# Where in SyncE's queue 32 loads for the gate rows of a two-layer diffusion block stand

## The chip, the core and the metric

The kernel runs on one core of one Trainium2 chip. The metric is the device time of one execution in microseconds (us), taken from several runs; beside it, one execution was recorded by the hardware profiler, and its span is the time from the first to the last instruction. In the rows of the profile PE is TensorE's matmuls, PEld its weight loads, DVE is VectorE, ACT is ScalarE, POOL is GpSimd and SP is SyncE; SPq and ACTq are the DMA queues that SyncE and ScalarE issue to. L439 is line 439 of the kernel.

## The reference

The reference is a small diffusion backbone of two layers over 256 latent tokens and 256 context tokens of width 1024, in float32. Each layer has a token mixer (a convolution module in layer 0, a bidirectional chunkwise mLSTM in layer 1) and a squared-ReLU MLP; each sub-layer is modulated, gated and normed. The modulation comes from one matrix per layer, applied to the latent condition `c` and to a learned context vector `c_ctx`:

```python
def adaln(cvec, w, b):
    return jnp.split(jax.nn.silu(cvec) @ w + b, 6, axis=-1)

for i in range(DEPTH):
    sh1, sc1, g1, sh2, sc2, g2 = adaln(c[:, None, :], ada_w[i], ada_b[i])
    csh1, csc1, cg1, csh2, csc2, cg2 = adaln(c_ctx, ada_w[i], ada_b[i])
    u, uc = modulate(h, sh1, sc1), modulate(hc, csh1, csc1)
    ...
    h = layer_norm(ALPHA * h + g1 * y, ln1_g[i], ln1_b[i])
    h = layer_norm(ALPHA * h + g2 * sq_relu_mlp(modulate(h, sh2, sc2), mlp_w1[i], mlp_w2[i]), ln2_g[i], ln2_b[i])
```

In layer 1 the mixer forms queries and keys from a convolved stream `xc`, values from `xm`, gates from all three, and an output gate `o`; then come attention over chunks, a norm per head, a down projection and the MLP. Layer 1 gives only the latent stream out, so of its gates only `g1` and `g2` of the latent condition are used. These two vectors of 1024 numbers are the "gate rows".

## The kernel before

**Products.** Weights arrive in blocks of 128 rows x 2048 columns of float32 (1 MB) by `raw_load` (L147 to L150) into one of three `raw` buffers. Each half of a block is split by `split_w` into a rounded high part (ScalarE's cast, `wh`, L155) and a remainder (VectorE's subtraction, `wl`, L156); four buffers of each exist. A product is three matmuls (high by high, high by low, low by high: L186, L189, L190; with other operand order L228 to L230). In the second layer's query stage it is two matmuls with operands side by side (L202). `raw_load` notes its DMA in `loaded[0]`: at any place of the program text that name stands for the weight load (or readback) written last.

**Stages around the change.** The MLP of layer 0 runs in four parts `c` of 1024 hidden columns: w1 in eight steps of 128 columns over 512 tokens, then relu on ScalarE (L1207), square on VectorE (L1208) and a split into `hid`; then w2, which adds into `x`. In the last part w2 runs over one half of the tokens after the other and keeps its later weights in `u` tiles. After it come the z and x halves of the up projection (`up_z`, `up_x`), the values (`wv`), and for each of two pairs of heads the queries (`queries`, `wq`) and the keys (`pair`, `wk`). In the keys each step of 128 rows is multiplied by the queries, split into `rr`, and one step later used by the scores (L1492 to L1497). Then come the output gate (`wo`), attention and the rest.

**The sums for the modulation of layer 1.** They are not matmuls. `AdaV` (L417 to L449) loads a block `adaT_w[unit, b, half]` of 128 columns of the modulation by 512 inputs (256 KB) into one of two `ar` buffers (L445, L446), and VectorE multiplies it by a broadcast row of silu(condition) and sums along the row in one instruction (L439), starting from the bias for the first half and from the first half's sum for the second. A unit is 512 columns, so it needs 8 loads. `ada_n1` sums four units for both conditions and is stepped in the MLP of layer 0. `ada_n2` sums eight units for the latent condition alone, in the order (6, 7, 8, 9, 4, 5, 10, 11): first shift and scale of the second sub-layer, then units 4, 5 (`g1`) and 10, 11 (`g2`). That makes 64 loads, numbered by `i`, and `n = i // 8`. Its steps are written into the program text at these places: 32 in the loop of `wv`, 4 in the queries of each head, 8 in the keys of each pair, and one at the end, after which `gate_rows` (L1255 to L1257) stores the two gate rows from their columns to DRAM, each as 1024 single numbers in another order. They are read back as rows, the first into `G` (L1650).

**What sets the order.** The framework that builds the kernel gives each engine its own list of instructions. It plans that order itself, from priorities that follow the program text and from its own estimate of when operands and buffers are ready; an instruction that is ready early may be placed far ahead of its place in the text. On the chip each engine then works its list in order and waits where an operand or buffer isn't ready. Two aids bind the plan: `tc.keep_in_program_order(ins)`, and `with tc.issue_after(ins):`, which puts the instructions of its block behind `ins` on the same engine's list. SyncE's list holds nearly all loads, weights and `ar` alike.

Of the kernel before, what the change touches and what calls it, by code (L numbers as in the profile page):

```python
# [71 lines left out]
def hybrid_kernel(ctx: ExitStack, tc: tile.TileContext, xT, vecs_d, taps_d, bdw_d, ada0_w, ada_w, adaT_w, wg_d, pw1a, pw1, pw2, w1_0, w2_0,  # L72
                  w1_1, w2_1, up_x, up_z, wv, wo, bo_d, wk, wq, wqT, wdown, rows_d, out):
    nc = tc.nc
# [10 lines left out]
    def nm(s):  # L85
        uid[0] += 1
        return f"{s}_{uid[0]}"
# [64 lines left out]
    loaded = [None]  # L152
# [9 lines left out]
    def split_w(src, make=None):  # L162
        n = src.shape[-1]
        if make is not None:
            his, los = [], []
            for i in range(0, n, T):
                his.append(make(F32R))
                los.append(make(F32R))
                split(his[-1], los[-1], src[:, i:i + T])
            return his, los  # L170
        hi = wp.tile([P, 1024], F32R, tag="wh", name=nm("wh"), bufs=NW)[:, :n]
        lo = wp.tile([P, 1024], F32R, tag="wl", name=nm("wl"), bufs=NW)[:, :n]
        anchors.append(split(hi, lo, src))
        return hi, lo
# [242 lines left out]
    class AdaV:  # L417
# [25 lines left out]
        def load(self):  # L443
            n, kt = divmod(self.i, DT)
            w = adp.tile([P, 512], F32, tag="ar", name=nm("ar"), bufs=2)  # L445
            nc.sync.dma_start(w, adaT_w[self.units[n], kt // 2, kt % 2])  # L446
            self.i += 1
            return w

# [1382 lines left out]
    def down(h):  # L1832
# [21 lines left out]
        if h == 0:  # L1854
            for hf, ws in enumerate(load()):
                for t in range(2):
                    ps = psum(("fl", "ln")[t])
                    mms(ps, ws, hf, t, True, True)
                    e_ = tmp("E")
                    nc.vector.tensor_tensor(e_, ps, G1[:, HF[hf]], op=ALU.mult)  # L1860
                    nc.vector.tensor_tensor(R[:, t, HF[hf]], R[:, t, HF[hf]], e_, op=ALU.add)
                    yield
        elif h < H - 1:
            if h == 1:
                acc.extend([[psum(), psum("fl")], [psum(), psum()]])
            for hf, ws in enumerate(load()):
                for t in range(2):
                    mms(acc[t][hf], ws, hf, t, h == 1, False)
                    yield
        else:  # L1870
            for t in range(2):
                for hf in range(2):
                    mms(acc[t][hf], pre3, hf, t, False, True)
                    with tc.issue_after(normed[0]) if t else nullcontext():
                        residual(t, hf, acc[t][hf], G1)
                    yield
                if t == 0:
                    normed.append(ln1_rows(0))
# [191 lines left out]
    for c in range(4):  # L2070
# [24 lines left out]
        for k2 in range(4):  # L2095
            raw = raw_load(w2_1[4 * c + k2])
            for i in range(2):
                kt = 2 * k2 + i
# [3 lines left out]
                w = split_w(raw[:, i * 1024:(i + 1) * 1024])  # L2102
                w = [[w_[:, sl] for sl in HF] for w_ in w]
# [127 lines left out]
```

## Time and profile before

| what | us |
|---|---|
| median of 3 runs | 1650.22 (1646.95 to 1651.23) |
| profiled execution | 1650.45 |
| its span | 1648.7 |
| 96 `ar` loads issued, first and last | 164.8 and 509.9 |
| 16 `wq` and 16 `wk` loads, median to landing | 4.8 |
| `ar` loads, median to landing | 3.0 |

The mean granted clock of TensorE over the span is 0.992. The stages in the order of time: layer 0's mixer to about 213 us, its MLP to about 585 us, the up projection to about 740 us, values to 912 us, queries and keys of the first pair to 1044 us, of the second to 1188 us, then output gate, attention, down projection and the MLP of layer 1.

A page of the profile names a group of instructions by line, engine, operation and its tiles (written tile, arrow, read tiles). In an order of time each row starts with the start and the length in us, and a bracket at its end gives the idle time of the engine before it and what released it. A row of windows gives the length, busy time and count of each engine, then the granted clock (1.00 is full speed), the share of the 16 DMA engines in use and GB/s. Although the steps of `ada_n2` are written into the values, queries and keys, the last of its loads was issued at 509.9 us, in the MLP of layer 0: the plan had placed them as soon as their operands were there.

### The profile page before, as it was taken

The page shows a single profiled execution, that of the slowest core. Times are in us where ns is not written, and L with a number is a line of the kernel's source. Part 1 is how long each engine was busy: PE and PEld are TensorE (multiplying, and loading weights), DVE is VectorE, ACT ScalarE, POOL GpSimd, SP SyncE. Part 2 cuts the span into 40 slices and gives each one's busy share as a digit, 9 for nine tenths or more (in the row PEclk, how much of TensorE's full clock was granted, in tenths as well). Part 3 has the DMA queues.
Part 4 walks back from the last instruction along what each step waited for, and adds up shares of the span by engine and source line. Part 5 has one row for each costly group of instructions (what it writes and reads, how often), then busy time and mean ns, then how long its engine had stood idle before and what let it go on. Part 6 is the DMA issues. An engine that isn't in the chain of part 4 may idle for free.

```text
span 1648.7 us, 22836 instructions
## 1 busy us (share of the span) xinstructions
PE 1623.7 (98%) x8754; PEld 1356.6 (82%) x8754; DVE 1077.0 (65%) x2052; ACT 728.1 (44%) x1173; POOL 15.2 (1%) x67
## 2 busy tenths in 40 slices
PE   9999999999996999999999999999999999999998
PEld 6675998888885998887777899898888888888887
DVE  7697886986756676763233643453389876787777
ACT  4214763322314376652222532442378654555453
POOL 0000000000000000000000000000000000000001
PEclk9999999999998999999999999999999999999999
DMA  9766233555655157578654632343375566745552
GB/s 361 250 220 239 103 115 128 197 190 193 201 176 153 52 164 226 188 242 281 220 188 149 238 128 103 107 175 131 136 258 187 209 230 203 255 182 190 191 192 90
DMA packets 91069, 306.88 MB, mean 186 GB/s; under 512 B 15020, under 2 KB 33360, under 8 KB 63312
## 3 DMA queue, kind: packets, MB, share of 16 engines
q1 hardware_dynamic: 66416, 289.12, 50.2%
q10 hardware_dynamic: 24544, 16.30, 3.2%
q8 instruction: 69, 1.13, 0.3%
q14 instruction: 40, 0.33, 0.1%
HBM read 287.52 MB, written 17.87 MB: 185 GB/s over the span
## 4 chain that ended last, share of the span: by engine, by line
PE 90%; DMA 6%; DVE 3%; issue 1%; ACT 0%; DVEq 0%; SPq 0%; ACTq 0%
PE mm L186 15%; PE mm L189 15%; PE mm L190 15%; PE mm L202 10%; DMA ar<-adaT_w 4%; PE mm L228 4%; PE mm L230 3%; PE mm L229 3%; PE cv L230 2%; PE cv L228 2%; PE cv L229 2%; PE fl L360 1%; DMA raw<-w 1%; DVE ar L439 1%; PE ln L228 1%; PE ln L229 1%
## 5 line engine op out<-in xcount | busy, mean ns | idle before, releaser
L156 DVE TENSOR_TENSOR wl<-raw,wh 128x1024 fp32r<-128x1024 f32 (+1 forms) x344 | 416.5, 1215 | 255.4 <-ACT wh L155 250.5
L155 ACT CAST wh<-raw 128x1024 fp32r<-128x1024 f32 (+1 forms) x344 | 357.0, 1045 | 458.8 <-PE mm L189 269.0
L189 PE MATMUL mm<-u,wh 128*128 128x512 f32 (+1 forms) x802 | 288.7, 361 | 0.0
L186 PE MATMUL mm<-u,wh 128*128 128x512 f32 (+1 forms) x674 | 239.3, 356 | 0.0
L190 PE MATMUL mm<-u,wl 128*128 128x512 f32 (+1 forms) x674 | 238.1, 355 | 0.0
L189 PEld LDWEIGHTS mm<-u,wh 128*128 128x128 f32 x802 | 151.2, 189 | 23.0 <-issue 0.8
L186 PEld LDWEIGHTS mm<-u,wh 128*128 128x128 f32 x674 | 127.2, 189 | 20.5 <-issue 2.4
L190 PEld LDWEIGHTS mm<-u,wl 128*128 128x128 f32 x674 | 127.1, 189 | 18.5 <-issue 0.8
L186 PE MATMUL mm<-hid,wh 128*128 128x512 f32 (+1 forms) x256 | 95.1, 372 | 13.4 <-ACT hid L155 13.3
L186 PE MATMUL mm<-xm,wh 128*128 128x512 f32 x256 | 100.2, 391 | 0.0
L190 PE MATMUL mm<-xm,wl 128*128 128x512 f32 x256 | 99.6, 389 | 0.0
L189 PE MATMUL mm<-hid,wh 128*128 128x512 f32 (+1 forms) x256 | 94.8, 370 | 0.7 <-DVE hid L156 0.7
L190 PE MATMUL mm<-hid,wl 128*128 128x512 f32 (+1 forms) x256 | 94.5, 369 | 0.0
L228 PE MATMUL mm<-wh,xl 128*128 128x512 f32 x208 | 81.5, 392 | 1.0 <-ACT xl L155 1.0
L229 PE MATMUL mm<-wh,xl 128*128 128x512 f32 x208 | 81.2, 390 | 0.0
L230 PE MATMUL mm<-wl,xl 128*128 128x512 f32 x208 | 80.4, 391 | 0.0
L189 PE MATMUL mm<-qq,wh 128*128 128x272 f32 x256 | 73.9, 289 | 0.0
L186 PE MATMUL mm<-qq,wh 128*128 128x272 f32 x256 | 73.5, 288 | 0.0
L190 PE MATMUL mm<-qq,wl 128*128 128x272 f32 x256 | 73.5, 288 | 0.0
L186 PEld LDWEIGHTS mm<-hid,wh 128*128 128x128 f32 x256 | 50.1, 196 | 21.6 <-ACT hid L155 14.1
L1373 DVE SCALAR_TENSOR_TENSOR E<-pad,vecs,E 128x512 f32<-128x512 f32 x64 | 48.0, 750 | 27.3 <-ACT E L1371 26.0
L155 ACT CAST hid<-E 128x256 fp32r<-128x256 f32 (+1 forms) x70 | 33.9, 485 | 67.9 <-DVE E L1208 64.4
(595 smaller groups left out, 3245.9 us busy)
## 6 DMA issues: line engine op xcount, KB each, us to landing
raw<-w SPq DMA_DIRECT2D x64, 1024.0 KB, 4.9
raw<-wo SPq DMA_DIRECT2D x32, 1024.0 KB, 4.9
ar<-adaT_w SPq DMA_DIRECT2D x96, 256.0 KB, 3.0
raw<-ada_w SPq DMA_DIRECT2D x20, 1024.0 KB, 7.4
raw<-wv SPq DMA_DIRECT2D x16, 1024.0 KB, 6.3
raw<-wq SPq DMA_DIRECT2D x16, 1024.0 KB, 4.8
raw<-wk SPq DMA_DIRECT2D x16, 1024.0 KB, 4.8
u<-wqT SPq DMA_DIRECT2D x56, 256.0 KB, 5.7
```

What stands on the lines that cost most here:

```text
L155: c = nc.scalar.copy(hi, src)
L156: lastsub[0] = nc.vector.tensor_tensor(lo, src, hi.bitcast(F32), op=ALU.subtract).ins
L186: a = nc.tensor.matmul(ps, wh, xh, start=start, stop=False)
L189: nc.tensor.matmul(ps, wh, xl, start=False, stop=False)
L190: lastmm[0] = nc.tensor.matmul(ps, wl, xh, start=False, stop=stop).ins
L202: nc.tensor.matmul(o_, w_, x_, start=start and i == 0, stop=stop and i == 15)
L228: nc.tensor.matmul(ps, xh, wh, start=start, stop=False)
L229: nc.tensor.matmul(ps, xl, wh, start=False, stop=False)
L230: return nc.tensor.matmul(ps, xh, wl, start=False, stop=stop).ins
L360: a = mark_unit[0] = nc.tensor.matmul(ps[32 * j:32 * j + 32], cs[:, kt, 14 - 2 * v:46 - 2 * v], blocks[kt], start=first and kt < 4, stop=l ...
L439: nc.vector.tensor_tensor_reduce(tmp("S") if s == 0 else w, w, crow[s][half], 1.0, o if half else V(f"ada_b{self.l}", col), op0=ALU.mult, ...
L1373: nc.vector.scalar_tensor_tensor(s2_(acc), pad[:, :, k:k + C], V("w_conv", m * QTAP + k), s2_(acc), op0=ALU.mult, op1=ALU.add)
```

## The change

```diff
         def load(self):
             n, kt = divmod(self.i, DT)
             w = adp.tile([P, 512], F32, tag="ar", name=nm("ar"), bufs=2)
-            nc.sync.dma_start(w, adaT_w[self.units[n], kt // 2, kt % 2])
+            with tc.issue_after(loaded[0]) if n > 3 else nullcontext():
+                nc.sync.dma_start(w, adaT_w[self.units[n], kt // 2, kt % 2])
             self.i += 1
             return w
```

`n > 3` never holds for `ada_n1`, which has four units. For `ada_n2` it holds for the last 32 loads, those of units 4, 5, 10 and 11. Each of them is placed on SyncE's list behind the load that `raw_load` wrote last before it in the program text. The load with `i = 32` is written in the last step of `wv`; those with `i` from 33 to 63 are written one per step in the queries and keys, so that behind nearly every `wq` and `wk` load comes one `ar` load. No instruction is added or removed, and the first 32 loads of `ada_n2` are bound to nothing, as before.

## The prediction

> **What bounds the kernel now.** I read the page's busy row and its slices first, to see whether one engine sets the time.
>
> ```profile
> span 1648.7 us, 22836 instructions
> ...
> PE 1623.7 (98%) x8754; PEld 1356.6 (82%) x8754; DVE 1077.0 (65%) x2052; ACT 728.1 (44%) x1173; POOL 15.2 (1%) x67
> ...
> PE   9999999999996999999999999999999999999998
> ```
>
> TensorE is busy in 98% of the span. A slice is 1648.7/40 = 41.2 us, and before the last only the thirteenth (494.6 to 535.8 us) is below 9. What can be won lies there. Two windows of the stages and two of TensorE alone say how much (busy time by engine, then granted clock, DMA share, GB/s):
>
> ```profile
> 428.00:519.00 91.00, 91.00 (x409) 75.56 (x408) 59.59 (x120) 25.05 (x33) 0.00 (x0) 1.00 0.57 183
> 519.00:545.00 26.00, 11.91 (x59) 10.72 (x58) 10.20 (x18) 6.82 (x11) 0.00 (x0) 0.61 0.59 162
> ```
>
> ```profile
> 521.00:533.00 12.00, 0.00 (x0) 0.60 0.75 172
> 533.00:535.00 2.00, 1.64 (x6) 0.50 0.02 8
> ```
>
> Up to 519 us TensorE never idles; then come 12 us without a matmul, and work resumes at a granted clock of 0.50. The view of TensorE's waits (total, times, longest) and its order of time name the cause:
>
> ```profile
> PE mm L186 <- ACT hid L155: 13.3, 2, 12.1
> PE mm L189 <- DVE hid L156: 0.7, 2, 0.3
> ```
>
> ```profile
> 533.04 0.58 PE L186 MATMUL mm<-hid,wh 128*128 128x256 f32 x1 [12.10 <-ACT hid L155]
> ...
> 537.67 0.58 PE L186 MATMUL mm<-hid,wh 128*128 128x256 f32 x1 [1.23 <-ACT hid L155]
> ...
> 543.38 0.41 PE L189 MATMUL mm<-hid,wh 128*128 128x256 f32 x1
> 543.60 0.37 PE L190 MATMUL mm<-hid,wl 128*128 128x256 f32 x1
> 543.80 0.28 PE L186 MATMUL mm<-hid,wh 128*128 128x256 f32 x1
> 543.92 0.28 PE L189 MATMUL mm<-hid,wh 128*128 128x256 f32 x1
> ```
>
> This is the start of the first layer's last w2 product, and it lacks the last blocks of hid. ScalarE makes them, and its queue stood at the cast of a weight load that had landed late; SyncE's queue shows why that load was issued late (x counts the loads of a row):
>
> ```profile
> 531.34 1.14 ACT L155 CAST u<-raw 128x512 fp32r<-128x512 f32 x2 [10.23 <-DMA raw<-w]
> ```
>
> ```profile
> L446 SPq DMA_DIRECT2D ar<-adaT_w x96: 327/328/425, 164.8 to 509.9; - x96
> ```
>
> ```profile
> 426.14 10.07 SPq L446 DMA_DIRECT2D ar<-adaT_w  x5
> ...
> 496.63 9.85 SPq L446 DMA_DIRECT2D ar<-adaT_w  x5
> 507.28 0.33 SPq L149 DMA_DIRECT2D raw<-w  x1
> 508.55 1.71 SPq L446 DMA_DIRECT2D ar<-adaT_w  x2
> 518.43 0.33 SPq L149 DMA_DIRECT2D raw<-w  x1
> ```
>
> Between weight loads stand up to five ar loads. Each waits for one of two ar buffers, so for a reduce on VectorE, which waits for an ar load in turn: five take 10 us, and the weights queue behind them. Counted back from the last of the 96, at 509.9 us, the 32 that the change moves begin with the group of 426.14 us (its first is the 64th or 65th of all). The whole stretch before the hole is theirs. The weight load of 518.43 us was slow besides:
>
> ```profile
> raw<-w SPq DMA_DIRECT2D x1, 1024.0 KB, 12.8
> raw<-up_z SPq DMA_DIRECT2D x1, 1024.0 KB, 14.1
> g_dr<-ada ACTq DMA_DIRECT2D x1, 4.0 KB, 11.1
> ```
>
> ```profile
> 516.70:527.80 11.10, 3.80 (x23) 3.00 (x22) 5.43 (x7) 2.27 (x4) 0.00 (x0) 0.80 0.50 28
> ```
>
> The first fence is the DMA view from 516 to 532 us (KB, us to landing), the second a window over the store of the second gate row. These 4 KB take 11.1 us, in which all DMA together moves 28 GB/s, against 183 in the stretch before; the load beside it landed after 12.8 us.
>
> **The change part by part.** It adds no instruction and removes none. It ties 32 loads of 256 KB to weight loads of the second layer: the first to the last load of the wv stage, the others to those of wq and wk (some to a readback of xc between them). Their 32 reduces move with them and, as they need the sums, the two stores.
>
> *What goes.* The waits: 13.3 + 0.7 = 14.0 us. The slow clock: it ends between 543.60 and 543.80, where the step from matmul to matmul falls from 0.22 to 0.12 us. From 533.04 to 543.6 are 10.6 us; less the 1.5 us of the later waits (13.3 + 0.7 without the 12.1 and one 0.3) they are 9.1, and the same matmuls at full clock save 9.1 x (1 - 0.12/0.22) = 4.1 us. Together 18 us, the most that can go.
>
> *What is late next.* A step of w1 is 24 matmuls of 0.22 us (91/409), 5.3 us. The load of 518.43 us needs the buffer that a split frees when TensorE is done with the step two before the last. Undelayed that is some 10 us before the hole and the load takes 5, so it would land some 5 us before it is needed: covered. Left over may be the last hid block, whose relu, square, cast and subtraction follow the last w1 matmul. It came 1.2 us late even after the weights had landed, with TensorE at half clock; its 3.1 us of work between 533.04 and 537.67 (4.6 less the 1.5 of waits) would be 1.7 at full clock, so the block would be 2.6 us late if nothing else moved. Below stands 0, since relu was itself queued behind the late weights. I take 1, the nearer row being the wait of 1.2.
>
> *What is added behind.* One reduce, the reads of the accumulator (count, then least, median and most ns), and two stages in which eight of each will stand (queries, then keys, of the first two heads; the other two heads alike):
>
> ```profile
> 443.48 0.75 DVE L439 CUSTOM_DVE_ANT_0 ar<-ar,L,vecs 128x512 f32<-128x512 f32 x1 [3.84 <-DMA ar<-adaT_w]
> ```
>
> ```profile
> L439 DVE DVE_READ_ACCUMULATOR2_ANT ada<- x128: 78/82/86, 260.7 to 516.6; 128x1 f32 x128
> ```
>
> ```profile
> 912.00:958.00 46.00, 46.00 (x266) 39.67 (x265) 28.52 (x47) 24.38 (x47) 0.00 (x0) 1.00 0.70 244
> 958.00:1044.00 86.00, 85.99 (x548) 78.92 (x547) 32.86 (x81) 26.76 (x49) 0.00 (x0) 1.00 0.29 104
> ```
>
> Eight times 0.83 (0.75 + 0.08) is 6.6 us for a VectorE that is busy 28.5 of 46 and 32.9 of 86 us. Eight loads are 2.1 MB, 46 GB/s more on 244, a DMA share of 0.70 x 290/244 = 0.83. The amounts are covered. The order is less sure: a reduce that waits for its load holds what stands behind it on VectorE, in the keys the subtraction that makes rr, and TensorE's scores wait for that. The bounds, from VectorE's waits before the reduces (us, times) and the margin of rr; the longest wait with no store near is the 3.84 us of the row above:
>
> ```profile
>   DMA ar<-adaT_w: 49.2, 28
> ```
>
> ```profile
> 1127.88 0.42 DVE L156 TENSOR_TENSOR rr<-mm,rr 128x256 fp32r<-128x256 f32 x1
> ```
>
> ```profile
> 1131.24 0.40 PE L186 MATMUL ln<-rr,u 128*128 128x512 f32 x1
> ```
>
> The 28 waits average 1.8 us; with the reduce that is 2.6. rr is done at 1128.30 and used at 1131.24, a margin of 2.9. So the usual wait is covered, and the longest (3.84 + 0.83 - 2.9) costs 1.8 us. Sixteen reduces fall to the keys: the bounds are 0 and 28 us. I take 1, near the usual wait.
>
> The Trainium skill speaks against the change here: its page "TensorE: Matmul & The Clock Gate" (the table at its head) calls VectorE's queue strict first in, first out, so no work can pass a waiting reduce; by that rule and the longest wait each time those 28 us are lost. The trace agrees, as VectorE idles before such a reduce with other work behind it.
>
> The stores keep their 11 us of slow DMA. The excess of the load beside one, 12.8 against a usual 4.9 in page part 6, is 7.9 us, the upper bound; the lower is 0, which I take: in the keys DMA is used at a share of 0.29, so the loads run ahead of TensorE. The gate rows are first wanted long after the keys:
>
> ```profile
> L1860 DVE TENSOR_TENSOR E<-fl,G x2: 683/688/692, 1340.8 to 1348.4; 128x512 f32<-128x512 f32 x2
> ```
>
> **Sum**, against the profiled run's own 1650.45 us (the span and 1.75 around it; the median of the runs shown is 1650.22): 1650.45 - 18 + 1 + 1 = 1634 us.
>
> **Rivals.** *The hole shrinks but stays* (0.08). If the w2 weights are late for another reason, say 4 us of waits stay, and with them the slow clock, for in the row of 521 to 533 us the clock of 0.60 means that it halved after 2.4 us without work (12 x 0.6 = 2.4 + 9.6 x 0.5). Price: 4 + 4.1, beside the 1 added behind: 1641. Against it stands the queue, where ar loads are in the way each time. On this the skill's page named above ("What's actually happening") has a busy window of about 3.4 us restore the clock; the clock term would then be 1.5 us (3.4 x 0.45, an estimate from that page). The trace differs, with some 10 us at half clock after work resumed, and it decides.
>
> *The waits move along* (slower, 0.08). One mechanism in one place: reduces in the keys hold up rr. It decides where a wait exceeds 2.1 us (2.9 - 0.83). If each of the sixteen waits the longest time, 28 us are lost against 18 won: 1650.45 - 18 + 28 = 1660. For it: an ar load will always stand behind 1 MB of weights. Against it: the mean of 1.8.
>
> *No change* (0.10). The same at a middling wait of about 3.1 us, 1 us lost in each of sixteen, gives the gain back: 1650. That the edge does nothing is excluded, as the earliest load it is tied to is one of the last wv loads:
>
> ```profile
> 855.87 11.21 SPq L149 DMA_DIRECT2D raw<-wv  x2
> ```
>
> **How the numbers follow.** The forecast, 0.74, is 1634, from 1632 (nothing left or added) to 1641 (2.6 left, 6 added). Eight times in ten: 1629 to 1648, three below for the spread of the runs (1646.95 beside the median of 1650.22), leaving out the slower case and most of no change. A measurement of this kernel can tell about 0.3%, 5 us. Faster 0.82 (the forecast and the first rival), within 0.3% 0.10, slower 0.08.
>
> **What would show it.** Right: no ar issue after about 430 us until wv ends, then one behind each weight load; TensorE without a hole from 519 to 545 us and its clock at 1.00; both stores after 950 us; the later stages as long as before, each some 16 us earlier. Wrong: idle time of TensorE before the scores with rr as releaser; a hole left near 520 us; a weight load of 12 us in the queries or keys with a cast waiting for it.

## The result and the profile after

| kernel | median us | runs | span of the profiled execution |
|---|---|---|---|
| before | 1649.62 (1646.95 to 1651.23) | 6 | 1648.7 |
| after | 1640.30 (1639.78 to 1641.55) | 6 | 1639.8 |

The ratio is 0.9945, with a 95% interval of 0.9932 to 0.9958. The change makes the kernel 9.3 us faster. The forecast was 1634 us, a gain of 16.

The page of the kernel after, span, busy row and slices:

```profile
span 1639.8 us, 22795 instructions
...
PE 1622.8 (99%) x8754; PEld 1355.0 (83%) x8754; DVE 1077.4 (66%) x2052; ACT 728.6 (44%) x1173; POOL 15.2 (1%) x67
...
PE   9999999999999999999999899999999999999998
```

The low slice has moved. The thirteenth is full, and the twenty-third is below 9. A slice is 41.0 us here, so the new gap lies between 902 and 943 us, in the first queries. Two windows show the old place, and the stage of values with the new one at its end (length, busy time of PE, PEld, DVE, ACT and POOL, granted clock, DMA share, GB/s):

```profile
519.00:545.00 26.00, 26.00 (x214) 25.61 (x213) 14.60 (x34) 5.82 (x12) 0.00 (x0) 1.00 0.22 82
...
740.00:912.00 172.00, 166.94 (x807) 128.90 (x806) 56.94 (x86) 47.14 (x78) 0.00 (x0) 0.99 0.59 199
```

TensorE is now busy through all 26 us where it had 11.9, at full clock. SyncE's list (start, length, issues) has become what the change asked for:

```profile
425.71 0.33 SPq L447 DMA_DIRECT2D ar<-adaT_w  x1
...
434.72 73.06 SPq L149 DMA_DIRECT2D raw<-w  x8
509.28 11.21 SPq L149 DMA_DIRECT2D raw<-up_z  x3
```

After the `ar` load of 425.71 us there are only weight loads, up to the first moved `ar` load at 848.24 us. The first `wq` load, which was issued at 884.75 us before, goes out at 865.86. Up to there the change has won 18.9 us, against the 18 of the working. So the hole did go, and the rest was given back later. TensorE's waits (total, times, longest) name the place:

```profile
PE mm L202 <- DVE xc L156: 5.0, 1, 5.0
PE cv L180 <- DVE ones L139: 1.1, 1, 1.1
PE mm L228 <- ACT xl L155: 1.0, 1, 1.0
```

These are the three longest. The second and third stood before too. The first is new. VectorE's order of time at that place, after:

```profile
900.51 0.75 DVE L439 CUSTOM_DVE_ANT_0 ar<-ar,L,ada 128x512 f32<-128x512 f32 x1 [4.28 <-DMA ar<-adaT_w]
901.19 0.08 DVE L439 DVE_READ_ACCUMULATOR2_ANT ada<- 128x1 f32 x1
907.38 0.75 DVE L439 CUSTOM_DVE_ANT_0 ar<-ar,L,vecs 128x512 f32<-128x512 f32 x1 [6.11 <-DMA ar<-adaT_w]
908.06 0.08 DVE L439 DVE_READ_ACCUMULATOR2_ANT ada<- 128x1 f32 x1
908.06 2.77 DVE L156 TENSOR_TENSOR xc<-raw,xc 128x256 fp32r<-128x256 f32 x8
```

Two reduces, each waiting for its load, stand on VectorE's list ahead of the eight subtractions that make the remainder of `xc`, the second layer's convolved stream. ScalarE had begun the high part at 900.31 us, so the subtractions could have started soon after. They started at 908.06. TensorE had run out of other work. Its first product with the high part of `xc` started at 908.87 us after 5.01 us without work.

In the kernel before the same subtractions waited for ScalarE alone:

```profile
918.79 2.77 DVE L156 TENSOR_TENSOR xc<-raw,xc 128x256 fp32r<-128x256 f32 x8 [3.66 <-ACT xc L155]
```

The loads behind the two reduces were issued at 896.70 and about 897.65 us. The DMA view of after from 896 to 902 us (issues, KB, median us to landing) shows what went out with them:

```profile
v_dr<-res ACTq DMA_DIRECT2D x4, 256.0 KB, 8.9
raw<-wq SPq DMA_DIRECT2D x1, 1024.0 KB, 7.7
ar<-adaT_w SPq DMA_DIRECT2D x2, 256.0 KB, 9.7
```

An `ar` load took 3.0 us at the median of the kernel before. The one of 897.65 us took 9.7, among 1 MB of weights and 1 MB of stores of the values. And the pause slowed the clock once more. Windows of after behind the wait:

```profile
908.00:911.00 3.00, 2.08 (x4) 0.88 (x4) 3.00 (x12) 0.00 (x0) 0.00 (x0) 0.68 0.00 1
911.00:914.00 3.00, 3.00 (x9) 2.42 (x9) 2.52 (x3) 1.68 (x4) 0.00 (x0) 0.50 0.69 227
914.00:917.00 3.00, 3.00 (x15) 2.62 (x14) 2.96 (x7) 1.77 (x6) 0.00 (x0) 0.68 1.01 412
```

The trace's clock records put the half clock from 909.09 to 915.92 us, 6.8 us. What it cost is read from the same products in both kernels, first after, then before:

```profile
908.87 2.80 PE L202 MATMUL mm<-xc,wh 128*128 128x512 f32 x4 [5.01 <-DVE xc L156]
...
911.69 1.91 PE L202 MATMUL mm<-xc,wh 128*128 128x512 f32 x4
...
916.42 2.00 PE L202 MATMUL mm<-u,wh 128*128 128x512 f32 x8
```

```profile
922.59 1.09 PE L202 MATMUL mm<-xc,wh 128*128 128x512 f32 x4
...
926.43 2.00 PE L202 MATMUL mm<-u,wh 128*128 128x512 f32 x8
```

From the first product with the high part of `xc` to the last row shown are 7.55 us after and 3.84 us before, so 3.7 us were lost behind the wait. The clock isn't all of it. The first four products took 2.6 us to the next row (908.87 to 911.47) and the four of 911.69 took 1.7, both at half clock: the subtractions, 2.77 us for all eight, were still being made while the first products used them. That this held the products up is read from the two rates; no run tried it alone.

So 18.9 - 5.0 - 3.7 = 10.2 should be left. The load of `G` goes out 9.8 us earlier than before and the end comes 8.9 us earlier (1648.7 - 1639.8). The last 1.3 us went in pieces below 1 us: three waits of TensorE behind this place that the kernel before doesn't have, of 0.7, 0.2 and 0.2 us, make up most of it.

### The profile page after: what moved, and what is told of

Its sections match the earlier page's. It is cut to its first block, busy times and chain, and to the rows that moved or that the text cites. A ratio compares the mean times of both kernels' runs of the same rounds, so it can differ in the third digit from the quotient of the medians.

```text
span 1639.8 us, 22795 instructions
## 1 busy us (share of the span) xinstructions
PE 1622.8 (99%) x8754; PEld 1355.0 (83%) x8754; DVE 1077.4 (66%) x2052; ACT 728.6 (44%) x1173; POOL 15.2 (1%) x67
## 4 chain that ended last, share of the span: by engine, by line
PE 95%; DMA 2%; DVE 2%; ACT 1%; issue 0%; SPq 0%; DVEq 0%; ACTq 0%
PE mm L186 18%; PE mm L189 18%; PE mm L190 18%; PE mm L202 8%; PE mm L228 3%; PE mm L229 3%; PE mm L230 3%; PE cv L228 2%; PE cv L230 2%; PE cv L229 2%; PE fl L360 1%; DMA ar<-adaT_w 1%; PE ln L186 1%; PE ln L229 1%; PE cv L964 1%; PE ln L230 1%
## 5 line engine op out<-in xcount | busy, mean ns | idle before, releaser
L186 PE MATMUL mm<-u,wh 128*128 128x512 f32 (+1 forms) x674 | 239.6, 356 | 0.0
L186 PEld LDWEIGHTS mm<-u,wh 128*128 128x128 f32 x674 | 127.3, 189 | 20.5 <-issue 2.4
L186 PE MATMUL mm<-xm,wh 128*128 128x512 f32 x256 | 100.2, 392 | 0.0
L186 PE MATMUL mm<-hid,wh 128*128 128x512 f32 (+1 forms) x256 | 93.1, 364 | 0.0
L189 PE MATMUL mm<-hid,wh 128*128 128x512 f32 (+1 forms) x256 | 92.8, 363 | 0.0
L186 PE MATMUL mm<-qq,wh 128*128 128x272 f32 x256 | 73.6, 289 | 0.0
L439 DVE CUSTOM_DVE_ANT_0 ar<-ar,L,vecs 128x512 f32<-128x512 f32 x48 | 36.0, 749 | 39.2 <-DMA ar<-adaT_w 38.9
```

Source lines behind the costliest of these rows:

```text
L186: a = nc.tensor.matmul(ps, wh, xh, start=start, stop=False)
L189: nc.tensor.matmul(ps, wh, xl, start=False, stop=False)
L439: nc.vector.tensor_tensor_reduce(tmp("S") if s == 0 else w, w, crow[s][half], 1.0, o if half else V(f"ada_b{self.l}", col), op0=ALU.mult, ...
```

## The experiments

The theory after reading: the hole is gone as forecast, and what is missing is one wait in the first queries plus the slow stretch behind it, since waiting reduces stand ahead of urgent work on VectorE. Two rivals: that the gate-row stores rather than the clogged list had made the old hole, so that moving them alone would do; and that any reduce in the queries and keys costs, so that fewer moved loads give proportionally more. All ratios are to the kernel before, run on the same chip. Its median was 1650.28 us (1648.86 to 1652.22, 7 runs) beside the first four kernels, and 1650.74 (1649.3 to 1652.8, 9 runs) beside the last three.

**1. The reduces behind the subtraction of xc.** The loads stay as in after. The reduces of the last four units are placed behind the last subtraction written before them.

```diff
+                with tc.issue_after(lastsub[0]) if self.units[n] in (4, 5, 10, 11) else nullcontext():
                     nc.vector.tensor_tensor_reduce(...)
```

> The changed kernel, with each moved reduce also put behind the last split written before it on VectorE's list; its loads stay where the change put them. Theory A (two reduces waiting for late ar loads stood ahead of the xc subtractions, and the first queries waited 5.0 us for those and then ran 6.8 us at half clock): the wait before the first products with xc goes, clock 1.00 there, 8 us gained on the changed kernel, about 1632. Rival B (the added loads crowd DMA in the queries, so weights and xc are late whatever stands on VectorE's list): the wait stays, about 1640.

Measured: 1637.84 us (1636.51 to 1639.01), ratio 0.9922 (0.9905 to 0.9938). That lies between theory A's 1632 and rival B's 1640, but the wait on `xc` is gone, as theory A has it. In its place comes another one, from ScalarE, at the start of the output gate. First PE, then ACT in the order of time of this kernel:

```profile
1184.59 0.50 PE L228 MATMUL mm<-wh,xl 128*128 128x512 f32 x1 [3.23 <-ACT wh L155]
```

```profile
1183.49 2.00 ACT L155 CAST wh<-raw 128x1024 fp32r<-128x1024 f32 x2 [4.29 <-DMA raw<-wo]
```

Its DMA view from 1168 to 1182 us:

```profile
raw<-wo SPq DMA_DIRECT2D x3, 1024.0 KB, 10.4
...
g_dr<-ada ACTq DMA_DIRECT2D x1, 4.0 KB, 9.6
```

With the reduces later, the second gate-row store comes later too, at 1168.62 us instead of 1136.0, and now stands beside the weight load that the output gate begins with. The 10.4 us are the median of the three `wo` loads. The first of them, issued at 1170.83 us, is the one that the cast waits for, and it took 12.6 us (the same view from 1170.5 to 1171.5 us). It is slow just as the load of 518.43 us was in the kernel before. So the wait on `xc` was due to the order on VectorE's list, and the price of a store, which the prediction bounded with 0 to 7.9 us, depends on which load it meets.

**2. Five loads left where they were.** Loads 32 to 36, those whose reduces come up before the subtraction of `xc`, are not bound. The other 27 are moved as in after.

```diff
-            with tc.issue_after(loaded[0]) if n > 3 else nullcontext():
+            with tc.issue_after(loaded[0]) if self.i > 36 and n > 3 else nullcontext():
```

> The changed kernel with the first five of the 32 loads left unbound, so that only 27 move; the lists from the first query on are those of the changed kernel. Theory A: no reduce stands ahead of the xc subtractions, the 5.0 us wait goes, and five loads more in the MLP still leave SyncE's queue free from about 437 us on, so no hole at 520: about 1632. Rival B (crowded DMA in the queries): 27 loads still stand there, about 1640.

Measured: 1632.14 us (1632.12 to 1632.60), ratio 0.9889 (0.9874 to 0.9904), 18.1 us faster than before and the fastest kernel of the study. All of TensorE's waits that the view lists:

```profile
PE cv L180 <- DVE ones L139: 1.1, 1, 1.1
PE mm L228 <- ACT xl L155: 1.0, 1, 1.0
```

Both stood in the kernel before. The old place and the keys in its windows:

```profile
519.00:545.00 26.00, 26.00 (x214) 25.61 (x214) 14.59 (x33) 5.96 (x13) 0.00 (x0) 1.00 0.22 82
...
958.00:1044.00 86.00, 86.00 (x525) 77.86 (x524) 37.71 (x90) 27.96 (x51) 0.00 (x0) 1.00 0.40 123
```

There is no half clock but in the last 6 us of the span, where every kernel here has one. This is the forecast's sum with nothing lost behind. Yet the reduces still wait. VectorE's waits of this kernel from 840 to 1190 us:

```profile
DVE ar L439 <- DMA ar<-adaT_w: 25.9, 14, 5.7
```

Fourteen waits, up to 5.7 us each, cost TensorE nothing. The wait of 5.0 us in after was a matter of place.

**3. Only the last sixteen loads moved.** Units 4 and 5 stay unbound; 10 and 11 are moved.

```diff
-            with tc.issue_after(loaded[0]) if n > 3 else nullcontext():
+            with tc.issue_after(loaded[0]) if n > 5 else nullcontext():
```

> The changed kernel with only the last 16 loads moved (units 10 and 11), the first store staying in the MLP. Theory A: SyncE's queue is free of ar loads from about 458 us on, with some 60 us left to fetch the last four weight blocks, so no hole at 520 and no reduce ahead of the xc subtractions: about 1632. Rival (each load taken from the old place wins its share, 18 us for 32): half the gain at 520, 9 us, about 1641. Rival (the first store alone can make a hole): some us of idle time near 480 to 520.

Measured: 1633.30 us (1632.86 to 1634.53), ratio 0.9897 (0.9882 to 0.9911). Moving sixteen loads gives nearly all that moving 27 gives. The first store stays in the MLP, at 470.4 us, and no hole follows. Its SyncE list:

```profile
459.40 7.59 SPq L447 DMA_DIRECT2D ar<-adaT_w  x4
468.58 40.16 SPq L149 DMA_DIRECT2D raw<-w  x5
510.24 11.21 SPq L149 DMA_DIRECT2D raw<-up_z  x3
```

From 468.58 us on the weights have the list to themselves, and that gives back enough lead. Kernel 2 is 1.2 us faster. An extra wait at the program's start, 1.8 us on the row `PE fl L360 <- DVE fold L719`, which the edit doesn't touch, is enough for that, but no run shows it to be the reason.

**4. Only the stores moved.** The kernel before, with all 64 loads where they were. The two gate-row stores are placed on ScalarE's list behind a late instruction of the second pair's keys.

```diff
+            with tc.issue_after(anchors[-1]):
-            nc.scalar.dma_start(g_dr[i].rearrange("(k p) -> p k", p=P), ada[1][:, u:u + 8, 1])
+                nc.scalar.dma_start(g_dr[i].rearrange("(k p) -> p k", p=P), ada[1][:, u:u + 8, 1])
```

> The kernel before, with only the two stores of the gate rows put behind the last key weights' cast on ScalarE's list; all ar loads stay in the MLP. Theory A with both causes (queue behind ar loads, and a load slowed from 4.9 to 12.8 us by the store): the weight load before the hole lands in about 5 us, the hole shrinks from 12.1 to 4 us, and the sum of wait and slow clock from 18 to 8: about 1640. Rival Q (the queue alone): 1650, the hole as before. Rival S (the store alone): no hole, 1632.

Measured: 1637.11 us (1635.74 to 1638.81), ratio 0.9919 (0.9904 to 0.9934). This misses the expectation: almost nothing of the hole is left, though no `ar` load was moved. First SyncE's list, then PE, in this kernel:

```profile
489.83 9.40 SPq L446 DMA_DIRECT2D ar<-adaT_w  x5
500.04 0.33 SPq L149 DMA_DIRECT2D raw<-w  x1
501.32 1.71 SPq L446 DMA_DIRECT2D ar<-adaT_w  x2
510.91 0.33 SPq L149 DMA_DIRECT2D raw<-w  x1
```

```profile
522.06 0.39 PE L186 MATMUL mm<-hid,wh 128*128 128x256 f32 x1 [0.51 <-ACT hid L155]
```

The list is as full of `ar` loads as before, but the last weight load goes out at 510.91 us instead of 518.43, and it lands after 4.7 us instead of 12.8. Together that is 15.6 us earlier. So the full list alone leaves half a microsecond of the hole; the stores were needed for it. What keeps this kernel 5 us behind kernel 2 is in part the same price in a new place: with both stores at 1143 us a `wo` load is late, and TensorE waits 2.0 us at 1162.13 us (`PE mm L186 <- DVE wgq L1518: 2.0, 1, 2.0`). The rest is small waits in several places (0.9, 0.7, 0.5 and 0.2), which were not followed up.

**5. Stores without the clog.** Kernel 2, with two stores added in the last part of the MLP, of the same kind and size as the gate rows' but to a buffer that nobody reads.

```diff
+    x_dr = dp.tile([2, D], F32, name="x_dr")
+
     def each1(c, m, s):
+        if c == 3 and m in (0, 6):
+            with tc.issue_after(mark["relu"]):
+                nc.scalar.dma_start(x_dr[m // 6].rearrange("(k p) -> p k", p=P), ada[1][:, 0:8, 1])
```

> The kernel of e2_five_loads_left (27 loads moved) with two more stores of 4 KB in single numbers, to a DRAM tile nobody reads, put on ScalarE's list in the last w1 product, near where the kernel before had its two stores. Theory C (a store makes a hole only where ar loads leave the weights without a lead): they cost nothing, as e2, 1632. Rival S (a store in the MLP costs by itself, since weight loads stand still for 11 us): 5 to 18 us, 1637 to 1650.

Measured: 1633.16 us (1632.51 to 1633.44), ratio 0.9894 (0.9879 to 0.9909). The stores were issued at 481.2 and 513.9 us. The first in this kernel's DMA view from 476 to 500 us, and the window over the second:

```profile
x_dr<-ada ACTq DMA_DIRECT2D x1, 4.0 KB, 11.7
```

```profile
514.00:526.00 12.00, 12.00 (x81) 10.94 (x80) 8.73 (x15) 5.99 (x10) 0.00 (x0) 1.00 0.61 95
```

The store is as slow as ever, the weight load that goes out while it runs lands after 7.8 us (the view from 483 to 490 us), and TensorE doesn't notice. So the stores alone don't make the hole either. It takes both: a weight load without lead, and a store beside it.

**6 and 7. One store at a time.** The kernel before, with only the second store placed late (6), and with only the first (7).

```diff
+            with tc.issue_after(anchors[-1]) if i else nullcontext():     (6)
+            with nullcontext() if i else tc.issue_after(anchors[-1]):     (7)
                 nc.scalar.dma_start(g_dr[i].rearrange("(k p) -> p k", p=P), ada[1][:, u:u + 8, 1])
```

> The kernel before with only its second store put behind the last key weights' cast; the first stays at about 469 us, all ar loads stay. Theory D (the two stores add: the first makes the last weight load issue 8 us late, the second makes it land 8 us late): the load is issued near 518 us and lands in 5, a hole of 4 to 5 us stays, clock halved or not, so a gain of 8 to 12: 1638 to 1642. Rival: the second store alone makes the hole, gain 13 as in e4, 1637.

> The kernel before with only its first store put behind the last key weights' cast; the second stays in the MLP, all ar loads stay. Theory D: the last weight load is issued near 511 us and lands in 12 to 13, a hole of 4 to 5 us stays, gain 8 to 12: 1638 to 1642. Rival: the second store alone makes the hole, no gain, 1650.

| kernel | median us | ratio | last weight load issued, landing after | longest wait in the hole |
|---|---|---|---|---|
| before | 1650.74 | | 518.43, 12.8 | 12.1 |
| 6, second late | 1643.13 (1642.31 to 1643.94) | 0.9955 (0.9940 to 0.9970) | 518.51, 4.7 | 4.0 |
| 7, first late | 1645.83 (1643.67 to 1646.63) | 0.9967 (0.9955 to 0.9980) | 513.80, 12.9 | 8.4 |
| 4, both late | 1637.11 (1635.74 to 1638.81) | 0.9919 (0.9904 to 0.9934) | 510.91, 4.7 | 0.5 |

The first store makes the last weight load go out late, the second makes it land late, and the two add. Both kernels gain less than was expected, though: 1643.13 and 1645.83 us lie above the 1638 to 1642 of theory D. In kernel 7 the last load went out at 513.80 us and not near 511, and the hole was 8.4 us instead of 4 to 5; why its list ran 2.9 us behind kernel 4's was not followed up. And the slow clock stayed, for 10.2 us in kernel 6 and 13.7 us in kernel 7. The store that was moved also has its price at the new place, as in kernel 4: 1.2 us of waiting in kernel 6 and 0.8 in kernel 7, on the row `PE mm L186 <- DVE wgq L1518`.

Why the first store, fifty microseconds earlier, still counts is seen in the DMA view of the kernel before from 468 to 485 us, and in VectorE's order there:

```profile
ar<-adaT_w SPq DMA_DIRECT2D x4, 256.0 KB, 10.0
raw<-w SPq DMA_DIRECT2D x1, 1024.0 KB, 12.0
g_dr<-ada ACTq DMA_DIRECT2D x1, 4.0 KB, 12.1
```

```profile
484.40 0.75 DVE L439 CUSTOM_DVE_ANT_0 ar<-ar,L,vecs 128x512 f32<-128x512 f32 x1 [7.57 <-DMA ar<-adaT_w]
```

The store holds up an `ar` load, the reduce waits 7.6 us for it, both `ar` buffers stay taken, and SyncE's list, which has three more groups of `ar` loads ahead of the last weights, never makes the delay good. In kernel 7 the second store stays. PE's order of time there:

```profile
528.47 0.58 PE L186 MATMUL mm<-hid,wh 128*128 128x256 f32 x1 [8.36 <-ACT hid L155]
```

The gains of 6 and 7, 7.6 and 4.9 us, add up to 12.5, against 13.2 in kernel 4 (1650.28 - 1637.11); the difference is within the spread of the runs.

## Why the prediction was right, and where it was off

- **What goes, 18 us (14.0 of waits, 4.1 of slow clock): right.** The first `wq` load comes 18.9 us earlier in after, 0.9 more than "the most that can go", and kernel 2, which loses nothing elsewhere, gains 18.1 us.
- **The cause, named as ar loads in the list ahead of weights: half of it.** Moving them removes the hole, but so does leaving them and moving the stores (kernel 4). The prediction quoted the store with its 11.1 us and 28 GB/s and the excess of 7.9 us, and set it down as "slow besides". It was a full partner, and the earlier store, which the prediction didn't quote, was another. That this term of the sum came out right is luck: the change happens to move all three.
- **What is late next, 1 us (0 to 2.6): 0.** TensorE is busy 26.00 of 26 us at the old place in after. The lower bound was right. In the kernel before, relu started at 534.89 us, on ScalarE right behind the casts of the late weights.
- **What is added behind, 1 us: this is the term that failed in size.** It cost 8.7 us, 5.0 of wait and 3.7 of slow products behind it, most of that half clock, for which the term had no price. The mechanism was named (a reduce waiting for its load holds what stands behind it on VectorE). That the 8.7 us lie within its bounds of 0 to 28 is luck, since these were worked out for sixteen reduces in the keys. The place was wrong: the working looked at `rr` in the keys, with its margin of 2.9 us, and not at the first queries, where the eight subtractions of `xc` stand behind two reduces. None of the three signs of being wrong that the prediction named showed up, because they too looked at the scores, the old hole and late weights. And the threshold was wrong. In the keys of after a reduce waited far longer than the 2.1 us that were to decide, and TensorE lost nothing there. VectorE's row and the window of the keys, after:

```profile
989.52 0.75 DVE L439 CUSTOM_DVE_ANT_0 ar<-ar,L,vecs 128x512 f32<-128x512 f32 x1 [5.34 <-DMA ar<-adaT_w]
```

```profile
958.00:1044.00 86.00, 86.00 (x534) 78.43 (x534) 36.79 (x90) 25.55 (x45) 0.00 (x0) 1.00 0.39 123
```

- That wait ran from 984.2 to 989.5 us and the matmuls went on throughout, so what stood behind the reduce on VectorE, a weight split at 990.20 us and `rr` at 991.34, was not needed sooner. The Trainium skill's rule from "TensorE: Matmul & The Clock Gate" (head table), that VectorE's queue is strict first in, first out, agrees with the row of 908.06 us, where the subtractions started 7.8 us after the casts that they need had begun (900.31). What the rule doesn't say is which wait costs.
- **The stores' slow DMA, 0 (up to 7.9): right for after**, where the stores go out at 974.5 and 1136.0 us. The `ar` load of the 5.34 us wait above had been issued beside the first of them and took 9.3 us, at no cost to TensorE. Kernels 1 and 4 show the other end: 3.2 and 2.0 us of waiting where a store meets the first `wo` loads.
- **The sum:** 1650.45 - 18.9 + 8.7 + 1.3 for small pieces gives 1641.55, which is what the profiled execution took. The small pieces are what is left over, so this is no check of the other terms.
- **The rivals.** "The hole shrinks but stays" gave 1641, close to the measured time, but by a mechanism that the window of 519 to 545 us excludes. "The waits move along" had the right kind of mechanism in the wrong place. Its place, the keys, didn't lose at all. "No change" fell as well: the gain is 0.55% (0.42 to 0.68).
- **The clock.** The prediction read about 10 us at half clock after work resumed and said that the trace differs from the Trainium skill's window of about 3.4 us ("What's actually happening", on the page named above). That reading counted from the first long wait and overlooked the short ones behind it. The last part below takes this up.

## What to carry to other kernels

Moving filler work out of a stage that had no lead won its whole hole here. But ask of each instruction that comes to wait on an in-order engine what stands behind it on that list at that place: a reduce's wait of 5.3 us cost nothing in the keys, and one of 6.1 us cost 8.7 in front of the one operand that TensorE had nothing to do without. A store of single numbers in another order is small only in bytes; put it where no load beside it is about to be needed, and if a prefetched stream runs without lead, look for such a store even 50 us upstream. When two causes sit in one row, undo each alone before giving one of them the whole sum.

## What the runs showed of the hardware that was not expected

**The clock moves on a fixed grid.** The trace's clock records of the kernels with a stretch at half clock before the tail:

| kernel | half clock, from and to, us | length | in steps of 3.413 | from the end of the last wait to full clock |
|---|---|---|---|---|
| before | 523.30 to 543.78 | 20.48 | 6 | 6.1 |
| after | 909.09 to 915.92 | 6.83 | 2 | 7.1 |
| 1 | 1186.00 to 1189.41 | 3.41 | 1 | 4.8 |
| 6 | 525.43 to 535.67 | 10.24 | 3 | 6.0 |
| 7 | 523.82 to 537.47 | 13.65 | 4 | 4.4 |

Each length is a whole number of 3.413 us, and so is each time from the first clock record to the slowing (518.83 = 152 steps before, 904.53 = 265 after, 1181.01 = 346 in kernel 1). This is what the Trainium skill's page "TensorE: Matmul & The Clock Gate" ("What's actually happening") calls a free-running window of 3413 ns, and the trace agrees. The last column counts from the last wait longer than 1 us. Work resumed in the kernel before at 533.04 us, and the full clock came 10.7 us later; short waits stood between, the last above 1 us ending at 537.67. A wait of 1.2 us in a recovering stretch seems enough to hold the clock down for another step; no run took such a wait away alone, so that is a reading. In the kernels before, 1, 6 and 7 the full clock came at the end of the first whole step behind that wait. In the kernel after it came one step later; there the first four products came at the slower rate until 911.47, within the step of 909.09 to 912.50, which may be the reason. One wait of 3.2 us was enough to slow the clock (kernel 1), and it did so 1.4 us after work had resumed; one of 2.0 us was not (kernel 4). In windows of kernel 6 the half clock looks like this (length, PE busy, clock, DMA share, GB/s):

```profile
526.00:530.00 4.00, 2.77 (x11) 0.50 0.45 143
530.00:536.00 6.00, 6.00 (x31) 0.53 0.67 257
536.00:545.00 9.00, 9.00 (x76) 1.00 0.01 2
```

**A 4 KB store of single numbers holds up the loads beside it.** Where a trace shows the landing of these stores, they took 9.3 to 12.1 us. The 1 MB weight loads beside one that TensorE came to wait for took 12.6 to 13.7 us (kernels before, 1, 4 and 7) instead of 4.7 to 4.9. The plainest pair is the kernel before and kernel 6, where the second store is moved and the same weight load goes out at 518.43 and 518.51 us: it lands after 12.8 us beside the store and after 4.7 without it. Its queue, `q10 hardware_dynamic` in the view of 468 to 485 us before, moved 1040 packets and held 3.4% of the engines' time, so the share of busy time doesn't show it. The time to landing of the loads beside it does. Why so few bytes hold up the others was not tried.
